# A decoder layer on eight cores: the first stage's norm without VectorE's reciprocal, loading in order of need, and a wider rope multiply

## The chip, the cores and the metric

The kernel runs on all 8 cores of one Trainium2 chip, 2,048 tokens to a core. The time is device microseconds of the slowest core. Each run has a state: it is slow when the cores of one die show a lower granted clock and take longer, or when the whole is over 1.5% above the fastest of its kernel. All medians given here are of fast executions alone; slow ones (a few per batch, up to 17% longer; in the longest, 1158.1 us, the cores of one die show a clock of 0.81 to 0.82, the others 0.99) are left out. Profiles are of one execution on its slowest core, so the core differs from run to run; the spans of the eight cores of a profiled run lie within about 1% of each other. Profiles of the kernel before carry buffer numbers in their names (`xsb_52_94`), the others do not (`xsb`).

PE is TensorE, ACT is ScalarE, DVE is VectorE, POOL is GpSimd, SP is the engine whose queue issues the token and table loads. PSUM is the memory that the matmuls of this program write to (`ps` in the profiles); a matmul that needs one of its buffers waits until the last result there has been read (in the kernel before TensorE's transposes wait 1.47 us, up to 69.09, for a v eviction).

## The reference

One decoder layer, cut to what the change touches:

```python
h = rms_norm(x, g_pre_mix)           # x * rsqrt(mean(x*x) + 1e-6) * g, row by row
proj = h @ w_in                      # q, k, v, pool input, gates
q = apply_rope(q); k = apply_rope(k) # [t1*cos - t2*sin, t2*cos + t1*sin]
# then three groups of dilated window attention, a pooling branch, gated merge,
# output projection, second norm, SwiGLU feed-forward
```

A core also computes k and v of the 2,048 tokens before its own (the halo), so its first stage normalises 32 tiles of 128 tokens: 16 own, 16 halo.

## The kernel before

The program is written as a list of operations; a small list scheduler, with an estimate of each operation's time, fixes the order of the instructions on every engine before the kernel is built. Engines then run their queues in that order and wait on semaphores.

The first stage, per tile: load 512 KB of tokens; sum of squares (ScalarE, for four early tiles VectorE); square root on ScalarE; reciprocal on VectorE; scaled copy to bf16 on ScalarE; eight transposes on TensorE; one VectorE multiply out of PSUM into `hT` (own) or `hTh` (halo). After every four tiles come the matmuls of q and k of the third head group (k alone for the halo), with rope, the rotation of q and k by position.

```python
def x_load(i):                       # token tile i; 8 own buffers, 5 halo buffers
    ...
    sp_x.append(sp.dma(t[:, :], src[j * 128:(j + 1) * 128, :]))

def tab(n):                          # rope table n (512 KB), two buffers, same SP queue
    while len(tab_t) < min(n + 2, len(tab_order)):
        t = tabs.new()
        sp.dma(t[:, :, :], tab_d[tab_order[len(tab_t)]], ahead=250, after=sp_x[-1:])
        ...

# norm of the first stage
act.activation(out=j[:, :], in_=src, func=AF.Square, accum_out=s_[:, 0:1])   # or a VectorE multiply
act.activation(out=s_[:, 0:1], in_=s_[:, 0:1], func=AF.Sqrt, scale=1.0 / D, bias=EPS)
dve.reciprocal(out=s_[:, 1:2], in_=s_[:, 0:1])
act.activation(out=xb[:, :], in_=src, func=AF.Copy, scale=rs)

# rope: b holds two 512-wide matmul results
for dst, fa, fb, op in ((dst_a, cos, sin, ALU.subtract), (dst_b, sin, cos, ALU.add)):
    t = rt.new()
    dve.tensor_tensor(out=t[:, 0, 0:n], in0=b[:, 0, 0:n], in1=fa, op=ALU.mult)
    dve.tensor_tensor(out=t[:, 1, 0:n], in0=b[:, 1, 0:n], in1=fb, op=ALU.mult)
    pool.tensor_tensor(out=dst, in0=view(t[:, 0, 0:n]), in1=view(t[:, 1, 0:n]), op=op)
```

Where the scheduler sees a hole of over 1 us on TensorE it puts filler matmuls on the identity.

The softmax here doesn't subtract the row's maximum and nothing guards it: scores larger than these inputs give would overflow.

## Time and profile before

| | before |
|---|---|
| time, median | 994.5 us |
| first q matmul | 25.0 us |
| last halo tile transposed | 108.0 us |
| first attention score matmul | 139.3 us |
| TensorE work needed and done by then | 97.9 us |
| TensorE time lost by then | 41.4 us |
| feed-forward (gate and up) begins | 517.8 us |

Lost time is the time of the first score less the needed matmuls before it at warm spacing (0.2157 us per 512 columns, 0.1092 per 256, 0.0556 per 128; in the kernel before, groups of eight stand at these spacings between 90 and 119 us, where the granted clock is 1.00). It counts matmul records of the timeline, rounded to whole groups of eight since a few records are missing. Fillers count as lost. The last halo tile is given by its last transpose (the prediction quotes the start of the same tile, 107.6 us).

From the page of the kernel before: the span, the busy times, and the chain that ended last by engine.

```profile
span 993.0 us, 15345 instructions; the slowest of 8 cores (989.5 to 993.0 us)
PE 929.5 (94%) x5574; PEld 474.3 (48%) x5574; DVE 380.8 (38%) x509; ACT 345.8 (35%) x556; POOL 364.8 (37%) x366
PE 79%; ACT 5%; POOL 5%; DVE 5%; issue 4%; DMA 1%; POOLq 0%; ACTq 0%; DVEq 0%; SPq 0%
```

TensorE bounds the whole, but "busy" includes fillers and matmuls at half clock (0.50 from 70 to 72 us). The stretches of the first stage show it; columns: stretch, its length, busy time of PE, weight load, DVE, ACT, POOL, granted PE clock, share of the DMA engines, GB/s.

```profile
40.00:50.00 10.00, 9.05 (x61) 4.58 (x62) 8.45 (x16) 9.65 (x18) 3.93 (x2) 1.00 1.02 288
50.00:60.00 10.00, 9.13 (x65) 4.85 (x63) 6.68 (x10) 9.53 (x18) 4.98 (x4) 1.00 0.41 109
60.00:70.00 10.00, 7.26 (x65) 4.88 (x63) 5.27 (x8) 9.73 (x19) 1.06 (x2) 0.95 0.83 216
70.00:80.00 10.00, 8.67 (x66) 6.67 (x65) 7.48 (x11) 5.21 (x11) 4.35 (x3) 0.88 1.02 263
```

DMA falls from full to 0.41 at 50 to 60 us, and PE's clock falls after it (0.95, then 0.88). The waits of the SP queue up to 138 us point to the cause; columns: who waited for whom, us in total, times, longest.

```profile
SPq L624 <- DVE rt_73_115 L635: 47.3, 5, 21.7
SPq L624 <- ACT xsb_52_94 L635: 38.2, 9, 18.6
SPq L624 <- ACT xsb_53_95 L635: 18.1, 8, 5.1
```

The queue stood 18.6 us for a free token buffer, until 60.4 us, and the third rope table stood behind that: it was issued at 61.90, after two token loads. From the timeline (start, length, what), the q matmuls of that table's unit, the table's issue, and its rope:

```profile
51.25 1.67 PE L637 MATMUL ps<-hT_68,wq_49_91 128*128 128x512 bf16 x7
...
61.90 0.39 SPq L635 DMA_DIRECT2D tab_70_112<-tab  x1
...
73.90 1.28 DVE L635 TENSOR_TENSOR rt_72_114<-ps,tab_70_112 128x512 f32<-128x512 f32 x2
```

The matmuls' result sat in PSUM for 20 us. And two tiles of the norm on ScalarE, from the timeline of that engine:

```profile
55.53 1.04 ACT L635 ACTIVATE junk_54_96<-xsth_44_86 128x1024 bf16<-128x1024 f32 x1
56.48 0.18 ACT L635 ACTIVATION_READ_ACCUMULATOR junk_54_96<-xsth_44_86 128x1 f32 x1
56.75 0.20 ACT L635 ACTIVATE st_9_51<-st_9_51 128x1 f32<-128x1 f32 x1
56.86 1.04 ACT L635 ACTIVATE junk_55_97<-xsth_45_87 128x1024 bf16<-128x1024 f32 x1
```

### The profile page before, as it was taken

To read this page: it belongs to the slowest core of one execution; us is meant where nothing else is said; L and a number is where in the kernel's file an instruction comes from. 1 tells how busy PE (TensorE), PEld (TensorE's weight loads), DVE (VectorE), ACT (ScalarE), POOL (GpSimd) and SP (SyncE) were. 2 spreads that over 40 slices of the span, in tenths; PEclk is the share of its full clock that TensorE was granted. 3 is DMA by queue.
4 is the path that set the end of the run, shared out by engine and by line. 5 is a ranking of instruction groups with operands and counts; after the bars stand their busy time and mean duration, and the time that the engine had idled before them with its cause. 6 is when DMAs were issued, how large, how long until landed. Compare 5 with 4: busy or idle time off the path is not lost.

```text
span 993.0 us, 15345 instructions; the slowest of 8 cores (989.5 to 993.0 us)
## 1 busy us (share of the span) xinstructions
PE 929.5 (94%) x5574; PEld 474.3 (48%) x5574; DVE 380.8 (38%) x509; ACT 345.8 (35%) x556; POOL 364.8 (37%) x366
## 2 busy tenths in 40 slices
PE   4989998979989999999889999999999999999992
PEld 2456776545554444444444444444444444444441
DVE  5768645677586334334453122111112111221111
ACT  4697446644446224224773111110101111111110
POOL 1528734646576435336882101102331000001322
PEclk9999999999999999999999999999999999999997
DMA  8968801310244334323876576662324444421221
GB/s 231 289 181 242 171 23 44 48 39 1 44 86 86 64 64 128 64 43 105 270 243 166 108 127 119 114 107 64 127 85 128 85 68 81 80 48 36 93 85 42
DMA packets 30778, 105.03 MB, mean 106 GB/s; under 512 B 3952, under 2 KB 3952, under 8 KB 30704
## 3 DMA queue, kind: packets, MB, share of 16 engines
q0 software_dynamic: 14432, 45.65, 27.2%
q1 hardware_dynamic: 15984, 58.33, 17.3%
q8 instruction: 46, 0.75, 0.3%
q14 instruction: 28, 0.23, 0.1%
q10 hardware_dynamic: 288, 0.06, 0.0%
HBM read 132.90 MB, written 16.78 MB: 151 GB/s over the span
## 4 chain that ended last, share of the span: by engine, by line
PE 79%; ACT 5%; POOL 5%; DVE 5%; issue 4%; DMA 1%; POOLq 0%; ACTq 0%; DVEq 0%; SPq 0%
PE ps L637 70%; PE ps L635 10%; DVE PT_75_117 L635 1%; ACT PT_75_117 L635 1%; DMA xst_37_79<-xo 1%; ACT xsb_53_95 L635 1%; POOL x1b_101_143 L635 1%; POOL x1b_102_144 L635 1%; ACT acc_70 L635 1%; POOL x1b_104_146 L635 1%; ACT junk_54_96 L635 1%; POOL x1b_103_145 L635 1%; ACT xsb_52_94 L635 0%; DVE PT_74_116 L635 0%; ACT junk_55_97 L635 0%
## 5 line engine op out<-in xcount | busy, mean ns | idle before, releaser
L637 PE MATMUL ps<-wdna_155,ffT_154 128*128 128x512 bf16 x512 | 115.7, 379 | 0.0
L637 PE MATMUL ps<-hT_68,wgu_109_151 128*128 128x512 bf16 x420 | 100.4, 379 | 0.0
L637 PE MATMUL ps<-hT_68,wgu_110_152 128*128 128x512 bf16 x420 | 100.4, 379 | 0.0
L637 PE MATMUL ps<-hT_68,wgu_111_153 128*128 128x512 bf16 x392 | 93.7, 379 | 0.0
L637 PEld LDWEIGHTS ps<-wdna_155,ffT_154 128*128 128x128 bf16 x512 | 50.1, 98 | 60.4
L637 PEld LDWEIGHTS ps<-hT_68,wgu_109_151 128*128 128x128 bf16 x420 | 41.0, 98 | 49.3
L637 PEld LDWEIGHTS ps<-hT_68,wgu_110_152 128*128 128x128 bf16 x420 | 41.0, 98 | 49.1
L637 PEld LDWEIGHTS ps<-hT_68,wgu_111_153 128*128 128x128 bf16 x392 | 38.3, 98 | 46.3
L637 PE MATMUL ps<-hT_68,wgs_76_118 128*128 128x512 bf16 x224 | 53.6, 379 | 0.6 <-ACT tg_80_122 L635 0.6
L637 PE MATMUL ps<-hT_68,wgs_77_119 128*128 128x512 bf16 x224 | 53.6, 379 | 0.0
L635 DVE TENSOR_TENSOR ffT_154<-ps,sa_115_157 128x512 bf16<-128x512 f32 x30 | 20.7, 691 | 79.2 <-PE ps L635 79.2
L635 DVE TENSOR_TENSOR ffT_154<-ps,sa_116_158 128x512 bf16<-128x512 f32 x29 | 20.0, 691 | 78.8 <-PE ps L635 78.8
L635 DVE TENSOR_TENSOR ffT_154<-ps,sa_117_159 128x512 bf16<-128x512 f32 x29 | 20.0, 691 | 76.7 <-PE ps L635 76.7
L635 ACT ACTIVATE sa_115_157<-ps 128x512 f32<-128x512 f32 x30 | 17.9, 597 | 80.4 <-PE ps L635 80.4
L635 ACT ACTIVATE sa_116_158<-ps 128x512 f32<-128x512 f32 x29 | 17.3, 596 | 80.9 <-PE ps L635 80.9
L635 ACT ACTIVATE sa_117_159<-ps 128x512 f32<-128x512 f32 x29 | 17.3, 596 | 78.0 <-PE ps L635 78.0
L635 ACT ACTIVATE junkd_107_149<-ps 128x1024 bf16<-128x1024 f32 x18 | 18.3, 1016 | 72.9 <-PE ps L635 72.8
L637 PE MATMUL ps<-wdnb_156,ffT_154 128*128 128x512 bf16 x160 | 39.8, 379 | 0.0
L635 ACT ACTIVATE junkd_108_150<-ps 128x1024 bf16<-128x1024 f32 x14 | 14.2, 1016 | 69.4 <-PE ps L635 69.4
L635 DVE SCALAR_TENSOR_TENSOR tg_80_122<-tg_80_122,ps 128x512 f32<-128x512 f32 x32 | 22.0, 687 | 42.7 <-ACT tg_80_122 L635 39.8
L635 POOL DMA_DIRECT2D wgu_109_151<-wgu x15 | 8.1, 540 | 81.9 <-PE ps L635 81.3
L635 DVE TENSOR_TENSOR PT_75_117<-PT_75_117,masks_44 128x1024 bf16<-128x1024 bf16 x24 | 32.2, 1343 | 14.8 <-ACT PT_75_117 L635 14.8
(499 smaller groups left out, 1821.2 us busy)
## 6 DMA issues: line engine op xcount, KB each, us to landing
wgu_109_151<-wgu POOLq DMA_DIRECT2D x15, 512.0 KB, 5.7
wgu_110_152<-wgu POOLq DMA_DIRECT2D x15, 512.0 KB, 5.7
wgu_111_153<-wgu POOLq DMA_DIRECT2D x14, 512.0 KB, 5.6
wgs_76_118<-wg POOLq DMA_DIRECT2D x8, 512.0 KB, 5.5
wgs_77_119<-wg POOLq DMA_DIRECT2D x8, 512.0 KB, 5.2
wdna_155<-wdn POOLq DMA_DIRECT2D x8, 512.0 KB, 8.4
tab_70_112<-tab SPq DMA_DIRECT2D x6, 512.0 KB, 6.0
tab_71_113<-tab SPq DMA_DIRECT2D x6, 512.0 KB, 7.3
```

The source lines that it names most:

```text
L635: e.ops.append(lambda q, m=method, a=a, k=k, s=sem.sem, v=step: getattr(q, m)(*a, **k).then_inc(s, v))
L637: e.ops.append(lambda q, m=method, a=a, k=k: getattr(q, m)(*a, **k))
```

## The change

Its intent: no hand-over to VectorE within the norm; tokens, tables and weights arriving in the order they are needed, with few loads in flight; later weights behind the tokens; one rope multiply over both halves. In it, `after=sp_x[-4:-3]` lets a token load start only when the fourth load before it is done, so at most four are in flight. The diff, cut to its core (`...` marks cuts):

```diff
-    xsb = P.ring("xsb", ... for i in range(2)], False)
-    junk = P.ring("junk", ... for i in range(2)], False)
+    xsb = P.ring("xsb", ... for i in range(4)], False)      # the square's waste goes here too
 ...
-        sp_x.append(sp.dma(t[:, :], src[j * 128:(j + 1) * 128, :]))
+        sp_x.append(sp.dma(t[:, :], src[j * 128:(j + 1) * 128, :], after=sp_x[-4:-3]))
+        if i % 4 == 3 and i > 3:
+            tab_load(sp_x[i - 3:i - 2])
 ...
-        pool.dma(wq2[:, c, :, :], wq_d[4 + c], d_w[c], after=[sp_x[1 + c]])
+        pool.dma(wq2[:, c, :, :], wq_d[4 + c], d_w[c], after=[sp_x[c]])
 ...  # wk likewise, after sp_x[2 + c] instead of sp_x[3]
-            act.activation(out=s_[:, 0:1], in_=s_[:, 0:1], func=AF.Sqrt, scale=1.0 / D, bias=EPS)
-            dve.reciprocal(out=s_[:, 1:2], in_=s_[:, 0:1])
+        act.activation(out=s_[:, 0:1], in_=s_[:, 0:1], func=AF.Ln, scale=1.0 / D, bias=EPS)
+        act.activation(out=s_[:, 1:2], in_=s_[:, 0:1], func=AF.Exp, scale=-0.5)
 ...
-        rs = rstd(t[:, :], True, i < 8 and i % 2 == 1)              # VectorE squares 4 tiles
+        rs = rstd_first(t[:, :], xb, i % 4 == 1 or i == 3)          # VectorE squares 9 tiles
 ...
-            dve.tensor_tensor(out=t[:, 0, 0:n], in0=b[:, 0, 0:n], in1=fa, op=ALU.mult)
-            dve.tensor_tensor(out=t[:, 1, 0:n], in0=b[:, 1, 0:n], in1=fb, op=ALU.mult)
+            dve.tensor_tensor(out=t[:, :, 0:n], in0=b[:, :, 0:n], in1=tf, op=ALU.mult)
 ...
-        if i >= NT and todo and i + 3 < 2 * NT:                     # later weights
+        if i + 6 >= 2 * NT and todo:
```

The change has three parts: **loads**, **norm** (with the four shared buffers and the nine VectorE squares) and **rope**.

More of the change, by code (lines that the diff above doesn't have):

```diff
@@ L771, in build_program @@
     wv2 = P.sb("wv2", [128, 8, 256], BF16, R3 + 24 * KB)
-    xsb = P.ring("xsb", [128, D], BF16, [R3 + 28 * KB + i * 2 * KB for i in range(2)], False)
-    junk = P.ring("junk", [128, D], BF16, [R3 + 32 * KB + i * 2 * KB for i in range(2)], False)
+    xsb = P.ring("xsb", [128, D], BF16, [R3 + 28 * KB + i * 2 * KB for i in range(4)], False)
     V01 = R3
@@ L823, in build_program, with tab_load @@
     tab_t = []
+    def tab_load(after, ahead=150):
+        t = tabs.new()
+        sp.dma(t[:, :, :], tab_d[tab_order[len(tab_t)]], ahead=ahead, after=after)
+        tab_t.append(t)
     def tab(n):
-        while len(tab_t) < min(n + 2, len(tab_order)):
-            t = tabs.new()
-            sp.dma(t[:, :, :], tab_d[tab_order[len(tab_t)]], ahead=250, after=sp_x[-1:])
-            tab_t.append(t)
+        while NT // 2 <= len(tab_t) < min(n + 2, len(tab_order)):
+            tab_load(sp_x[-1:], 250)
         return tab_t[n]
@@ L838, in build_program @@
     for c in range(2):
-        pool.dma(wq2[:, c, :, :], wq_d[4 + c], d_w[c], after=[sp_x[1 + c]])
-    tab(0)
+        pool.dma(wq2[:, c, :, :], wq_d[4 + c], d_w[c], after=[sp_x[c]])
+    tab_load([sp_x[0]])
     for c in range(2):
-        pool.dma(wk2[:, c, :, :], wk_d[4 + c], d_w[2 + c], after=[sp_x[3]])
+        pool.dma(wk2[:, c, :, :], wk_d[4 + c], d_w[2 + c], after=[sp_x[2 + c]])
     xt += [x_load(i) for i in range(4, 10)]
@@ L859, in build_program, with rstd_first @@
     P.filler = (any1, warm)
-    def rstd(src, first=False, by_dve=False):
-        s_, j = st.new(), junk_ring[0].new()
+    def rstd_first(src, j, by_dve):
+        s_ = st.new()
         if by_dve:
@@ L867, in rstd @@
             act.activation(out=j[:, :], in_=src, func=AF.Square, accum_out=s_[:, 0:1])
-        if first:
-            act.activation(out=s_[:, 0:1], in_=s_[:, 0:1], func=AF.Sqrt, scale=1.0 / D, bias=EPS)
-            dve.reciprocal(out=s_[:, 1:2], in_=s_[:, 0:1])
-            return s_[:, 1:2]
+        act.activation(out=s_[:, 0:1], in_=s_[:, 0:1], func=AF.Ln, scale=1.0 / D, bias=EPS)
+        act.activation(out=s_[:, 1:2], in_=s_[:, 0:1], func=AF.Exp, scale=-0.5)
+        return s_[:, 1:2]
+    def rstd(src):
+        s_, j = st.new(), junk_ring[0].new()
+        act.activation(out=j[:, :], in_=src, func=AF.Square, accum_out=s_[:, 0:1])
         pool.tensor_scalar(out=s_[:, 0:1], in0=s_[:, 0:1], scalar1=D * EPS, scalar2=None, op0=ALU.add)
@@ L874, in rstd @@
         return s_[:, 1:2]
-    junk_ring = [junk]
+    junk_ring = [None]
     def to_feature_major(src, rs, ring, xb, gain, dst):
@@ L897, in rope @@
         b = ring.new()
-        cos, sin = tb[:, 0, t0:t0 + n], tb[:, 1, t0:t0 + n]
+        f = tb[:, 0, t0:t0 + n]
         mm8(b[:, 0, 0:n], wa, rhs)
         mm8(b[:, 1, 0:n], wb, rhs)
-        for dst, fa, fb, op in ((dst_a, cos, sin, ALU.subtract), (dst_b, sin, cos, ALU.add)):
+        for dst, swap, op in ((dst_a, False, ALU.subtract), (dst_b, True, ALU.add)):
             t = rt.new()
-            dve.tensor_tensor(out=t[:, 0, 0:n], in0=b[:, 0, 0:n], in1=fa, op=ALU.mult)
-            dve.tensor_tensor(out=t[:, 1, 0:n], in0=b[:, 1, 0:n], in1=fb, op=ALU.mult)
+            tf = tb[:, 1, t0:t0 + n].fap([(-512, 2), (1, n)]) if swap else f.fap([(512, 2), (1, n)])
+            dve.tensor_tensor(out=t[:, :, 0:n], in0=b[:, :, 0:n], in1=tf, op=ALU.mult)
             pool.tensor_tensor(out=dst, in0=view(t[:, 0, 0:n]), in1=view(t[:, 1, 0:n]), op=op)
@@ L963, in build_program @@
         t = xt.pop(0)
-        rs = rstd(t[:, :], True, i < 8 and i % 2 == 1)
+        xb = xsb.new()
+        rs = rstd_first(t[:, :], xb, i % 4 == 1 or i == 3)
         j = (i % NT) * 128
-        to_feature_major(t[:, :], rs, any1, xsb.new(), gpre, (hT if i < NT else hTh)[:, :, j:j + 128])
+        to_feature_major(t[:, :], rs, any1, xb, gpre, (hT if i < NT else hTh)[:, :, j:j + 128])
         if i >= NT and i + 5 < 2 * NT:
@@ L982, in build_program @@
             todo += [(wu[:, c, :, :], wu_d[c]) for c in range(2)] + [(wq01[:, c, :, :], wq_d[c]) for c in range(4)]
-        if i >= NT and todo and i + 3 < 2 * NT:
+        if i + 6 >= 2 * NT and todo:
             d, w = todo.pop(0)
-            pool.dma(d, w, dsem("d_w01_%d" % len(todo)), after=[sp_x[i + 3]])
+            pool.dma(d, w, dsem("d_w01_%d" % len(todo)), after=[sp_x[i]])
     sp.dma(masks[:, :, :], masks_d[:, :, :], dsem("d_masks"), after=[sp_x[-1]])
```

## The prediction

> **What bounds the kernel now.** TensorE: busy 94% of the 993 us span, 79% of the chain that ended last. The change touches almost only the stage before attention (first attention score matmul at 139.3 us in the timeline) and the rope multiplies beside attention.
>
> In those 139 us TensorE does, counted from the timeline at its warm spacing (1.72 us per eight 512-column matmuls, 0.87 us per eight of 256, 0.44 us per eight transposes), about 98 us of needed work, 7 us of it pulled forward from the next stage. Some 41 us are lost: 12 us until the first tile is normalised, 10 to 12 us of filler matmuls on the identity, waits, and cold clock (near 70 us eight 256-column matmuls take 1.7 us).
>
> **Why.** First q matmul at 25.0 us: ScalarE's Copy of tile 3 waits until 21.2 us for a reciprocal that stands in VectorE's queue behind an eviction and a square of 1.2 us each; the same costs 4.7 us near 33 us. Then the load queue: the waits of SP show 18.6 us (41.8 to 60.4) on a free token buffer, with the third rope table behind it, issued at 61.9 us. Its q unit, multiplied at 51 to 54 us, gets its factors at 74 us and holds PSUM meanwhile. DMA falls to 0.41 share in 50 to 60 us, from 1.0 before. The last halo tile is transposed at 107.6 us; 31 us of matmuls follow.
>
> **What the change does.**
> - The reciprocal (VectorE, 0.15 us, 32 times, two hand-overs) becomes an Exp on ScalarE (0.1 us of step). VectorE squares 9 tiles instead of 4 (1.2 us each). ScalarE per tile: 2.4 us becomes 2.5, or 1.4 where VectorE squares; mean 2.2. [...] the attention's Ln and Exp run from 205 to 296 us without a table load. The load at 140 us (1.28 us) should go.
> - Four shared bf16 buffers instead of two: Copies run further ahead.
> - Loads in order of need: first q at 18 to 21 us (4.5 MB at 280 GB/s), no table behind a blocked token load.
> - Rope: a pair of 512-wide multiplies (1.29 us) becomes one 1024-wide, estimated at 1.22 us (what 128x1024 evictions take), but starts only when both matmul groups are done. About nothing.
>
> **Sum.** ScalarE: 7.4 us start + 32 x 2.2 + 10 us of v evictions gives 88 us; DMA: 21 MB of tokens and tables and 3 MB of early weights give 83 to 86 us. So the last halo tile at 92 to 98 us instead of 107.6, then the same tail: 10 to 16 us less before attention, about 4 us given back as less is pulled forward. About 1 us from the table load. The gain is on TensorE's critical path; what comes after is bound by TensorE and just shifts.
>
> I predict 982.5 us, 8 times in 10 between 972 and 991. Faster by over 2%: 0.15; within 2%: 0.83; slower by over 2%: 0.02.
>
> **Right if:** first q matmul near 20 us; no SP wait over 8 us; ropes within 4 us of their matmuls up to 70 us; first attention scores at 124 to 132 us; one table load fewer; the rest of the span unchanged within 4 us.
> **Wrong if:** four token loads in flight hold DMA well under 1.0 share before 80 us; ScalarE's serial chain Square, Ln, Exp, Copy is not overlapped between tiles; late weights make the first local keys wait; TensorE refills the hole in attention with more waits or a lower granted clock.

## The result

The kernel after takes 995.2 us (994.5 to 995.8), the kernel before 994.5. The ratio of the means is 1.0008, 95% interval 0.9991 to 1.0026: no difference. (A ratio here is the mean time of one kernel's fast runs over that of the other's of the same rounds, so not quite the ratio of the medians quoted.)

| | before | after | predicted |
|---|---|---|---|
| first q matmul, us | 25.0 | 20.0 | 18 to 21 |
| last halo tile transposed | 108.0 | 109.7 | 92 to 98 |
| first attention score | 139.3 | 138.2 | 124 to 132 |
| needed TensorE work by then | 97.9 | 92.7 | about 4 less |
| lost TensorE time by then | 41.4 | 45.5 | not stated |
| first score to feed-forward | 378.5 | 379.6 | shifts only |
| feed-forward to end | 475.2 | 475.1 | unchanged |

So the gain was not given back later. It never came about: the first stage loses 4 us more than before. (The rows from the trace are of the slowest core. Among the eight cores of one execution the lost time spreads by 2 to 8 us; the median of the eight is 39.6 before and 44.4 after, so the difference stands.) The page of the kernel after, the same three lines:

```profile
span 992.9 us, 15230 instructions; the slowest of 8 cores (989.8 to 992.9 us)
PE 921.5 (93%) x5490; PEld 473.1 (48%) x5582; DVE 381.6 (38%) x427; ACT 348.1 (35%) x577; POOL 370.3 (37%) x366
PE 75%; issue 6%; POOL 5%; ACT 4%; DMA 4%; DVE 4%; SPq 0%; ACTq 0%; POOLq 0%; DVEq 0%
```

The stretches of its first stage:

```profile
30.00:40.00 10.00, 7.83 (x59) 4.10 (x57) 8.67 (x10) 7.17 (x16) 5.31 (x3) 1.00 0.62 202
40.00:50.00 10.00, 8.39 (x60) 4.52 (x62) 6.34 (x7) 9.08 (x18) 2.00 (x2) 1.00 1.01 281
50.00:60.00 10.00, 9.35 (x62) 4.80 (x61) 8.46 (x9) 6.24 (x12) 9.17 (x5) 1.00 0.59 236
60.00:70.00 10.00, 7.29 (x49) 3.45 (x48) 9.83 (x10) 8.95 (x18) 5.40 (x3) 1.00 0.42 150
70.00:80.00 10.00, 7.87 (x64) 4.53 (x66) 8.91 (x9) 9.08 (x18) 4.08 (x3) 1.00 0.76 227
```

The clock is full now, but from 40 to 80 us PE is less busy (32.9 us against 34.1), DMA is full in one stretch only, and ACT is at 0.9 in three of the five. The SP queue's waits up to 138 us:

```profile
SPq L624 <- DVE rt L635: 54.4, 6, 27.4
SPq L624 <- DMA xst<-xo: 31.1, 12, 6.2
SPq L624 <- ACT xsb L635: 30.4, 12, 8.7
```

The long wait for a token buffer is gone (18.6 us down to 8.7); tables still wait for ropes. One tile and the Square of the next, from ScalarE's timeline (the line with x2 is Ln and Exp):

```profile
64.55 1.04 ACT L635 ACTIVATE xsb<-xsth 128x1024 bf16<-128x1024 f32 x1
65.49 0.19 ACT L635 ACTIVATION_READ_ACCUMULATOR xsb<-xsth 128x1 f32 x1
65.77 0.50 ACT L635 ACTIVATE st<-st 128x1 f32<-128x1 f32 x2
66.36 1.15 ACT L635 ACTIVATE xsb<-xsth,st 128x1024 bf16<-128x1024 f32 x1
67.42 1.04 ACT L635 ACTIVATE xsb<-xsth 128x1024 bf16<-128x1024 f32 x1
```

Square, read-out, Ln, Exp and Copy of one tile now stand one behind the other, each waiting for the last: 67.42 - 64.55 = 2.87 us a tile. Ln and Exp take 66.36 - 65.77 = 0.59 us. And ScalarE waits for squares that VectorE does. Its two largest waits up to 110 us, after that for the very first load:

```profile
ACT st L635 <- DVE xsb L635: 7.7, 3, 4.0
ACT xsb L635 <- DMA xst<-xo: 6.5, 2, 4.2
```

The longest of the first line, in VectorE's timeline and then ScalarE's:

```profile
29.46 1.22 DVE L635 TENSOR_TENSOR rt<-ps,tab 128x1024 f32<-128x1024 f32 x1 [3.37 <-PE ps L635]
30.60 1.21 DVE L635 SCALAR_TENSOR_TENSOR xsb<-xst 128x1024 bf16<-128x1024 f32 x1
...
31.91 0.50 ACT L635 ACTIVATE st<-st 128x1 f32<-128x1 f32 x2 [4.00 <-DVE xsb L635]
```

The square at 30.60 stood in VectorE's queue behind a rope multiply that waited 3.37 us for TensorE.

### The profile page after: what moved, and what is told of

It reads as the page before. It is cut to its first block, busy times and chain, and to the rows that moved or that the text cites. A ratio compares the mean times of both kernels' runs of the same rounds, so it can differ in the third digit from the quotient of the medians.

```text
span 992.9 us, 15230 instructions; the slowest of 8 cores (989.8 to 992.9 us)
## 1 busy us (share of the span) xinstructions
PE 921.5 (93%) x5490; PEld 473.1 (48%) x5582; DVE 381.6 (38%) x427; ACT 348.1 (35%) x577; POOL 370.3 (37%) x366
## 4 chain that ended last, share of the span: by engine, by line
PE 75%; issue 6%; POOL 5%; ACT 4%; DMA 4%; DVE 4%; SPq 0%; ACTq 0%; POOLq 0%; DVEq 0%
PE ps L637 66%; PE ps L635 9%; POOL x1b L635 3%; ACT xsb L635 2%; POOL st L635 1%; DMA wk<-wk 1%; DVE rt L635 1%; DMA xst<-xo 1%; DMA xsth<-xh 1%; ACT st L635 1%; DVE x1b L635 1%; ACT acc L635 1%; DMA gfin<-gfin 1%; DVE PT L635 0%; ACT PT L635 0%
## 5 line engine op out<-in xcount | busy, mean ns | idle before, releaser
L637 PE MATMUL ps<-hT,wgu 128*128 128x512 bf16 x1203 | 290.8, 379 | 1.2
L637 PEld LDWEIGHTS ps<-hT,wgu 128*128 128x128 bf16 x1232 | 120.4, 98 | 144.7
L635 DVE TENSOR_TENSOR ffT<-ps,sa 128x512 bf16<-128x512 f32 x88 | 60.9, 692 | 234.6 <-PE ps L635 234.6
L637 PE MATMUL ps<-wdna,ffT 128*128 128x512 bf16 x502 | 115.2, 379 | 0.5
L637 PE MATMUL ps<-hT,wgs 128*128 128x512 bf16 x434 | 106.1, 379 | 2.2 <-DVE zT L635 1.0
L635 DVE TENSOR_TENSOR rt<-ps,tab 128x1024 f32<-128x1024 f32 (+1 forms) x60 | 70.6, 1192 | 47.8 <-PE ps L635 35.6
L635 POOL TENSOR_TENSOR x1b<-x1b,xin 128x1024 f32<-128x1024 f32 x32 | 74.9, 2346 | 33.1 <-DVE x1b L635 31.6
L635 POOL TENSOR_TENSOR k<-rt 128x512 bf16<-128x512 f32 (+1 forms) x36 | 67.1, 1871 | 34.8 <-DVE rt L635 34.6
L635 POOL TENSOR_TENSOR q<-rt 128x512 bf16<-128x512 f32 x24 | 53.8, 2253 | 60.6 <-DVE rt L635 56.7
L635 DVE TENSOR_TENSOR PT<-PT,masks 128x1024 bf16<-128x1024 bf16 x48 | 57.3, 1206 | 26.4 <-ACT PT L635 26.0
L635 PE MATMUL ps<-hT,wgu 128*128 128x512 bf16 x176 | 66.7, 379 | 0.3
```

What stands on the lines that cost most here:

```text
L635: e.ops.append(lambda q, m=method, a=a, k=k, s=sem.sem, v=step: getattr(q, m)(*a, **k).then_inc(s, v))
L637: e.ops.append(lambda q, m=method, a=a, k=k: getattr(q, m)(*a, **k))
```

## The experiments

Theories: **A**, the norm in one serial chain on ScalarE eats what the loads gain. **B**, the throttled loads starve the stage. **C**, the rope has a part in it. All 18 kernels were correct; each was timed in five rounds against the kernel before on the same chip, which took 994.0 to 994.5 us.

### Each part alone on the kernel before

The edits: only the rope lines of the diff (`b_rope`), only the norm lines with the buffers and nine squares (`b_norm`), only the load lines (`b_load`).

> The kernel before with the 1024-wide rope multiplies alone. Theory 1 (the change's first stage costs TensorE about 5 us, and something beside attention gives it back): if the rope is what gives back, this alone is 3 to 6 us faster than before, with the first attention scores near 139 us and the gain between 140 and 320 us. Rival (the giving back was only the granted clock, or the order of the list scheduler): within 2 us of before.

> The kernel before with the norm's part alone: Ln and Exp on ScalarE, 9 squares on VectorE, four shared bf16 buffers; old loads, old rope. Theory A (the serial Square, Ln, Exp, Copy on ScalarE, 2.87 us a tile in the trace after against about 2.45 before, is what eats the gain): ScalarE tiles again near 2.9 us, last halo transposes no earlier than 106 us, total within 3 us of before or slower. Theory B (the loads eat it): ScalarE not the limit, first scores some us earlier, total 4 to 8 us faster.

> The kernel before with the loads' part alone: at most four token loads in flight, tables in order, later weights behind the tokens; old norm, old rope. Theory A (norm eats): first q near 20 us, the 18.6 us wait of the load queue gone, last halo transposes by 102 us, total 4 to 8 us faster. Theory B (throttled loads starve the stage): DMA share under 0.7 between 30 and 70 us as in the trace after, ScalarE waiting for tokens, total within 3 us of before or slower.

Measured: rope alone 999.9 us (ratio 1.0066), norm alone 1004.1 (1.0100), loads alone 985.4 (0.9912). Norm alone transposed its last halo tile at 116.6 us and lost 50.5 us before attention; loads alone did so at 102.5 and lost 39.8. This went for theory A. ScalarE with the new loads and the old norm, in the kernel with the loads alone:

```profile
37.70 1.04 ACT L635 ACTIVATE junk<-xst 128x1024 bf16<-128x1024 f32 x1
38.64 0.19 ACT L635 ACTIVATION_READ_ACCUMULATOR junk<-xst 128x1 f32 x1
38.74 1.13 ACT L635 ACTIVATE xsb<-xst,st 128x1024 bf16<-128x1024 f32 x1
39.77 0.19 ACT L635 ACTIVATE st<-st 128x1 f32<-128x1 f32 x1
39.87 1.04 ACT L635 ACTIVATE junk<-xst 128x1024 bf16<-128x1024 f32 x1
```

A tile takes 39.87 - 37.70 = 2.17 us, and the square root 0.10 us of it, because the Copy of another tile stands between a tile's Square and its root. That is a tile in the best case. Over the whole stage I summed ScalarE's steps, from the start of one instruction to the start of the next, without its waits of over 0.15 us: the norm of the 32 tiles takes ScalarE 70.6 us with the loads alone (2.21 a tile) and 81.0 us in the kernel after (2.53), 10.4 us more. On the other side, with the loads alone ScalarE waits 15.8 us for VectorE's reciprocals (12 times), which the change removes.

The rope alone was slower than I expected, and my rival did not foresee it. Its trace shows a stall of TensorE near 70 us; the kernel before has shorter ones there:

```profile
67.05 0.27 PE L635 MATMUL ps<-wv,hT 128*128 128x256 bf16 x1
71.72 0.91 PE L637 MATMUL ps<-ident,xsb 128*128 128x128 bf16 x7 [4.40 <-ACT v L635]
...
75.34 1.69 PE L637 MATMUL ps<-wv,hT 128*128 128x256 bf16 x7
```

With the old loads a table again came late: its rope began at 69.9 us, 14 us after its matmuls, and held PSUM till then. The gap of 4.4 us itself ended with v evictions on ScalarE, which stood in its queue behind a Square that had waited 2.1 us for a token load. After these 4.4 us of idleness seven 256-column matmuls took 1.69 us instead of 0.93 (75.34 against 65.41). But no unbroken gap of that length came before such a stretch in the kernel before: there seven of them at 69.90 took 1.70 us, at a granted clock of 0.50 from 70 to 72 us, after gaps of only 1.23 and 1.47 us with one group of transposes between them (TensorE was busy 0.61 us from 65.78 to 69.09). Why the clock falls after such gaps is not shown. Whether the wide multiply itself caused the longer stall or only the order did is taken up below.

### ScalarE's steps interleaved

The kernel after with one line of the scheduler's model changed; instructions the same (fillers aside), order different:

```diff
-  lat = ... (0.0 if e is self.pe else self.SELF)                     # SELF = 0.06 us
+  lat = ... (0.0 if e is self.pe else (0.3 if e is self.act and n.idx < self.first_end else self.SELF))
```

> The kernel after, with the same instructions; only the list scheduler is told that a dependent step on ScalarE in the first stage takes 0.3 us instead of 0.06 us to become ready, so that it puts another tile's Square or Copy between Square, Ln, Exp and Copy of one. Theory A: a ScalarE tile falls from 2.87 us to about 2.4 us, last halo transposes from 109.7 to about 100 us, total 5 to 9 us faster than after (986 to 990). Theory B (loads): ScalarE then waits for tokens instead, total within 3 us of after.

Measured: 989.2 us, 6.1 less than the kernel after; last halo tile at 101.0 us, lost time 39.3; the norm takes ScalarE 71.3 us (2.23 a tile) instead of 81.0. For theory A. ScalarE in this run:

```profile
73.18 1.04 ACT L635 ACTIVATE xsb<-xsth 128x1024 bf16<-128x1024 f32 x1
74.13 0.19 ACT L635 ACTIVATION_READ_ACCUMULATOR xsb<-xsth 128x1 f32 x1
74.22 0.39 ACT L635 ACTIVATE st<-st 128x1 f32<-128x1 f32 x2
74.52 1.13 ACT L635 ACTIVATE xsb<-xsth,st 128x1024 bf16<-128x1024 f32 x1
```

Here Ln and Exp belong to different tiles and take 74.52 - 74.22 = 0.30 us instead of 0.59. With the read-out of the sum it is alike: 0.09 us to the next instruction here (74.13 to 74.22) and 0.10 with the loads alone (38.64 to 38.74), but 0.28 in the kernel after (65.49 to 65.77), where the next reads the sum.

TensorE, the engine that bounds the whole, shows the same. Its waits for ScalarE's Copies from 15 us to the first score, in the kernel after and then interleaved:

```profile
PE ps L637 <- ACT xsb L635: 10.7, 15, 1.1
```

```profile
PE ps L637 <- ACT xsb L635: 1.2, 2, 0.8
```

With the loads alone this wait is 3.4 us, in the kernel before 3.6.

### Parts taken out of the kernel after

The kernel after without its norm (`l_rope`), without its rope (`a_norope`), and with Ln and Exp alone put back to Sqrt and reciprocal (`a_recip`).

> Loads and rope parts, old norm (the kernel after without its norm). The rope alone cost 6.6 us on the old loads, where a late table held PSUM and TensorE went cold near 70 us. Theory 1 (the rope's cost was that stall, an interaction): on the new loads it costs nothing, total 983 to 988. Theory 2 (the 1024-wide multiply is itself worse, as it waits for both matmul groups): about 992, 6 us slower than the loads alone (985.4).

> Loads and norm parts, old rope (the kernel after without its rope). Theory 1 (the norm on ScalarE costs 10 us wherever it stands): within 3 us of the kernel after (992 to 998). Rival (on the new loads the norm is harmless and the rope costs): near 986.

> The kernel after with Ln and Exp put back to Sqrt on ScalarE and the reciprocal on VectorE; its 9 squares on VectorE, four buffers, loads and rope stay. Theory A (Exp in ScalarE's serial chain costs): a ScalarE-squared tile falls from 2.87 to about 2.2 us, total 985 to 989. Rival (the 9 squares on VectorE, caught behind rope multiplies, cost): within 3 us of the kernel after.

Measured: 991.0, 995.3 and 991.7 us. On the new loads the norm costs 4.2 us with the rope and 10.0 without it. Putting back Ln and Exp alone gives 3.6 us, less than the 6 to 10 that theory A had: ScalarE's waits for reciprocals come back with them (18.9 us). The nine squares with their buffers make no difference that shows there (991.7 with them, 991.0 without). The rope costs 5.6 us on the loads alone and nothing on loads with norm. The parts do not add up (by their ratios alone 6.6 + 9.9 - 8.7, so 7.8 us slower; it was 0.8), which made me doubt what single runs say.

### More table buffers

The loads alone, with three buffers more for the first seven tables, in space whose weights come later:

```diff
+    tabs1 = P.ring("tab1", [128, 2, 512], F32, [R4, R4 + 4 * KB, R4 + 24 * KB])
-        t = tabs.new()
+        t = (tabs1 if len(tab_t) < NT // 2 - 1 else tabs).new()
```

A first build, which is not in the record, let a weight overwrite the eighth table, which is read once more later; the check refused it before any run.

> Loads part alone plus three rope table buffers of the first stage (in space whose weights come later) beside the two old ones, so that no table load blocks the token loads behind it. Theory (the 0.47 DMA share at 30 to 40 us is the token loads standing behind a table that waits 6.5 us for VectorE): no wait of the load queue on rope multiplies before 90 us, DMA share over 0.8 at 30 to 40 us, 2 to 5 us faster than the loads alone (980 to 983). Rival (that hole is already covered by work queued on TensorE and ScalarE, or ScalarE is the limit there): within 1.5 us of 985.4.

The stretch at 30 to 40 us, with the loads alone and then with the table buffers:

```profile
30.00:40.00 10.00, 8.61 (x60) 4.25 (x58) 7.99 (x13) 6.80 (x13) 5.51 (x4) 1.00 0.47 161
```

```profile
30.00:40.00 10.00, 8.59 (x62) 4.44 (x61) 7.87 (x15) 8.01 (x15) 6.07 (x4) 1.00 1.02 318
```

The hole in the DMA is filled, as the theory had it, and nothing is won: the first score comes at 132.6 us as against 132.4, lost time 39.1 as against 39.8. Missing DMA share between 30 and 40 us was no bottleneck; theory B fails there. But the whole took 991.3 us, 5.9 more than the loads alone. In the profiled executions the loss arose after the first score (380.1 us from there to the feed-forward against 375.8), where nothing was changed except the order of instructions.

### Controls: the same work in other orders

One number of the scheduler's model (how long until another engine sees a result) at 0.13 or 0.07 instead of 0.10 us. Needed work, data and buffers stay; only the order and the fillers differ, and the order of TensorE's queue differs by about as many lines as it does for a real part of the change.

```diff
-    LAT = 0.1
+    LAT = 0.13      # or 0.07
```

> Control: the kernel before, same work, with one number of the list scheduler's model (time for a result to be seen by another engine) at 0.13 instead of 0.10 us, so only the order of instructions differs. If orders of equal worth differ by little, within 2 us of before (992 to 996); then the 6.6 us of the rope and the 5 us of the table buffers have causes of their own. If the order alone is worth 5 us or more, no single run below that size says anything about its part of the change.

> The same disturbance on the loads part alone (985.4). If the 8.7 us gain of the loads is theirs: 983 to 988. If the first run was a lucky order: near 990, as with the three table buffers.

> The same disturbance on loads plus rope (991.0). If the 1024-wide multiply costs 5 us on the new loads by itself, again 4 to 7 us above the disturbed loads alone. If that was luck of the order: within 3 us of them.

> The same disturbance on the kernel after (995.2). The norm's cost comes from ScalarE's chain in every order: again 992 to 999, and 4 us or more above the disturbed loads plus rope. If it comes near them, the norm's cost was luck of the order too.

> The kernel before in a third order (the scheduler's number at 0.07). Two orders gave 994.1 and 985.6. If 994 is typical and 985.6 lucky: 990 to 996. If before as it stands was unlucky: 984 to 989. TensorE time lost before the first attention score 41 to 46 us.

> The loads part alone in a third order. Two gave 985.4 and 989.2. If loads help in every order: 983 to 990, lost time before attention 38 to 42 us.

> The kernel after in a third order. Two gave 995.2 and 997.6. If the norm's serial steps on ScalarE cost in every order: 993 to 999; a result under 990 would say that its cost too was luck.

> The kernel after with ScalarE's steps interleaved, in a second order (0.13). The first gave 989.8. If interleaving mends the norm: 985 to 991 and below the kernel after in the same order (997.6) by 5 us or more; ScalarE's step per tile near 2.3 us again.

Medians in us, and in brackets the lost TensorE time before the first score:

| | order 0.10 | order 0.13 | order 0.07 |
|---|---|---|---|
| before | 994.5 (41.4) | 985.6 (44.0) | 999.1 (50.4) |
| loads alone | 985.4 (39.8) | 989.1 (41.6) | 987.9 (40.6) |
| loads and rope | 991.0 (41.8) | 990.5 (38.9) | not run |
| after | 995.2 (45.5) | 997.6 (41.5) | 1000.4 (50.5) |
| after, interleaved | 989.2 (39.3) | 991.4 (37.9) | not run |

The lost times are of the slowest core. The medians of the eight cores, in the same three orders, are 39.6, 43.0 and 47.1 before, 37.3, 39.1 and 38.4 for the loads alone, 44.4, 41.1 and 43.9 after, 38.3 and 37.3 interleaved.

Of the eight expectations, those for the kernel after and the loads and rope in the order 0.13 (the latter as luck of the order) and for the loads in the order 0.07 came out as stated. The interleaved kernel came out 6.2 us below the kernel after but just above its range; the loads in the order 0.13 fell between their two cases; the kernel before in the order 0.13 fell into the case that the control was made for, an order worth over 5 us; in the order 0.07 it and the kernel after came out above their ranges.

The kernel before moved over 13 us by order alone. That is more than anything I had predicted. In the order 0.13 it lost more time in the first stage than as delivered (44.0 against 41.4), and yet came out 8.9 us faster: from the first score to the feed-forward it took 364.3 us instead of 378.5, with 12.2 us of TensorE's waits there instead of 23.6. Every other kernel here took 374 to 385 us, so this is one lucky order. So that stretch, in which I had said everything "just shifts", depends on order more than the first stage does.

What stands apart from this spread:

- The kernel after is slower than the loads alone in each order, by 9.8, 8.5 and 12.5 us, and the two sets do not overlap (985.4 to 989.1, 995.2 to 1000.4). Norm and rope together cost about 10 us. Not all of it arises where I had looked: on the slowest cores the first score comes later by 5.8, 0.0 and 9.9 us, and the stretch from there to the feed-forward is longer by 3.8, 6.6 and 5.5 us. That second share is not explained.
- Interleaving gives back about 6 us in both orders tried (6.1 and 6.2), and there it is the first score that comes earlier, by 6.3 and 3.7 us. What the interleaved kernel still lacks against the loads alone (3.8 and 2.3 us) lies after the first score.
- TensorE's waits for Copies before the first score: 10.7, 9.7 and 11.2 us in the three orders of the kernel after; 3.6, 3.6 and 5.6 before; 3.4, 3.6 and 1.7 with the loads alone; 1.2 and 3.2 interleaved. With Ln and Exp alone put back it is 3.8. So the norm's chain reaches TensorE in every order.
- The norm costs in every pair measured: 4.2, 7.1 (loads and rope against after), 10.0 (without rope) and about 10 on the old loads. Its sign is the same each time; its size is within what order alone does.

What does not stand apart:

- The loads' gain over the kernel before: 9.1 and 11.2 us in two orders, a loss of 3.5 in the third. They do lose less TensorE time in the first stage in all three (by 1.6, 2.4 and 9.8 us; by the medians of eight cores 2.3, 3.9 and 8.7).
- The rope's cost: 6.6, 5.6, 1.4 and nothing, and a gain in the next run. Its cause was argued from one stall and is not shown.

### A version that beats both

Two last runs, one after the other, undo one thing each from the interleaved kernel: the old rope back (`self_norope`), then no square on VectorE (`self_norope_dve0`, so that the norm is indeed ScalarE's alone).

```diff
-        rs = rstd_first(t[:, :], xb, i % 4 == 1 or i == 3)
+        rs = rstd_first(t[:, :], xb, False)
```

> Loads and norm with ScalarE's steps interleaved, old 512-wide rope. Interleaved with the new rope: 989.8. If the 1024-wide rope costs here too (5.6 and 1.7 us on the loads in two orders): 984 to 988. If that was luck of the order: 988 to 993.

> The same with no square on VectorE. If the waits of ScalarE on squares held in VectorE's queue (9.0 us in the interleaved run, longest 4.1) count: 2 to 5 us faster than the run before it, ScalarE waiting for VectorE in the norm not at all. If ScalarE is the limit after 50 us: 9 more squares of 1.04 us on it, slower by 3 to 8 us, last halo transposes after 105 us.

Measured: 992.5 us, so the old rope is 3.3 slower here; then 985.1 us, 7.4 less where 2 to 5 were expected (ratio to the kernel before 0.9904, interval 0.9888 to 0.9919). ScalarE's waits up to 110 us in the first of the two had this line on top:

```profile
ACT st L635 <- DVE xsb L635: 14.0, 6, 6.3
```

In the second no wait for VectorE in the norm remains. The last halo tile is transposed at 97.8 us and the lost time is 34.0 us, the least of all runs and 3.9 us below the next. That the squares cost is suggested by this one pair, in one order only: the 7.4 us of the total lie within what order alone does, but the wait, the time of the last tile (107.5 to 97.8 us) and the lost time (41.8 to 34.0; medians of eight cores 39.6 to 33.6) move together. As a whole, 985.1 us beats both kernels as delivered, yet is no better than the loads alone (985.4) or the old kernel in a lucky order (985.6).

## Why the prediction was wrong

Point by point, in the prediction's order.

1. **What bounds the kernel, and where the 41 us go: right.** Counted again with the rule above: 97.9 us needed, 41.4 lost.
2. **"ScalarE per tile: 2.4 us becomes 2.5 ... mean 2.2": wrong, and the step that failed.** The Exp was costed at 0.1 us, an estimate; it is the step that the Sqrt has in the kernel before, where another tile's Square follows (0.11 us, 56.75 to 56.86). In the schedule that was built, Ln follows the Square it reads, Exp follows Ln, and Copy follows Exp. The tile took 2.87 us. With 23 tiles at 2.87 and 9 at 1.63 the mean is 2.52, so 32 tiles take 81 us, not 70. The prediction named this among its dangers ("not overlapped between tiles") but gave it no weight. Undoing it by order alone gave back about 6 us, twice. The whole of the prediction's sum for ScalarE, up to the end of the last Copy, against what the timelines show (us):

   | | predicted | after | before | loads alone |
   |---|---|---|---|---|
   | start | 7.4 | 6.9 | 7.4 | 7.6 |
   | table load | none | 1.3 | 1.3 | 1.3 |
   | norm of 32 tiles | 70 | 81.0 | 71.3 | 70.6 |
   | v evictions before the end | 10 | 1.7 | 3.9 | 2.0 |
   | waits | none | 14.2 | 23.1 | 20.4 |
   | end of the last Copy | 88 | 105.1 | 107.2 | 102.0 |

   So the sum failed in two terms: the norm's own steps, and waits, for which it had no term (after: 7.7 us for squares on VectorE, 6.5 for tokens). It was helped by chance, as most v evictions came later than it had them. The change did cut ScalarE's waits (23.1 to 14.2 us), but the chain took as much again. And the last tile's transposes began only 4.2 us after its Copy had ended, behind four groups of v matmuls that stood before them in TensorE's queue.
3. **"VectorE squares 9 tiles" as a relief: wrong.** It took work off ScalarE but put ScalarE behind VectorE's queue, where ropes wait for TensorE: 7.7 us of waits in the kernel after, up to 14.0 in a variant. I had found just this mistake in the kernel before, with the reciprocal, and did not ask where else it would come back.
4. **Loads: the mechanism was right, the size not.** First q at 20.0 us as predicted, the 18.6 us wait gone, the first rope multiplies within 4 us of their matmuls up to 70 us, lost time less in every order with the loads alone. "No SP wait over 8 us" was wrong (8.7, and 27.4 late in the stage). DMA did fall well under 1.0 share, my first "wrong if"; but filling that hole at 30 to 40 us won nothing there. Late weights, another "wrong if", cost TensorE 1.9 us of waits.
5. **Table load: right.** The load at 140 us is gone; six loads up to 400 us instead of seven. From 6.93 to 296.2 us the kernel after, which runs the norm's and the attention's Ln and Exp in that time, shows no load between.
6. **Rope: the instruction was right, its worth is open.** The wide multiply takes 1.219 us, predicted 1.22. Across pairs it went from a gain of 3.3 to a loss of 6.6 us, within what order alone does.
7. **"What comes after ... just shifts": right for this pair, wrong as a rule.** It held for this pair (378.5 and 379.6 us from the first score to the feed-forward), but not in general: in that stretch runs took from 364 to 385 us. The feed-forward to the end, 475 to 478 us, is what shifts.

The range was wrong too: it took no account of the order of instructions, which was worth 13 us for the same work.

Open: why the kernel after and the interleaved one are slower than the loads alone after the first score; how much of the kernel before's 994.5 us is an unlucky order; whether the wide rope helps or hurts; and which waits in the attention stretch make 364 or 385 us of it.

## What to carry to other kernels

A small step moved onto the engine that holds its neighbours takes less there with other work between the dependent steps (Ln and Exp 0.30 us, against 0.59 back to back); cost it by its step in the chain that will be built, not by its duration, and interleave two tiles by hand or by telling the scheduler what a dependent step costs. Do not hand a step of a tight chain to an engine whose queue holds instructions that wait for something slower (ScalarE waited 7.7 us, in a variant 14.0, for VectorE's squares). Where a scheduler fixes the order, time the unchanged kernel in a few orders first (985.6 to 999.1 us here for the same work): differences below that spread are not findings. A stage's lost time and the waits of its bottleneck engine, read from the trace on several cores, tell more of that stage than the total does.
